# Row-normalising kernel, one core: in the first tile VectorE scales 7 of 12 rows and ScalarE 5, in place of 8 and 4

## The chip, the cores and the metric

The kernel runs on one core of a Trainium2 chip. The metric is the device time of one execution in microseconds (us). Before the change the median was 317.5 us (three runs, 316.85 to 318.54).

## The reference

```python
x = np.random.randn(32, 512, 1024).astype(np.float32)   # seeded

def reference(x):
    sums = np.sum(np.abs(x), axis=-1, keepdims=True)
    return (x / (sums + 1e-8)).astype(np.float32)
```

There are 16,384 rows of 1024 fp32 numbers, each divided by the sum of its absolute values. 67.11 MB are read and 67.11 MB written; every byte is used once.

## The kernel before

The rows go through 11 tiles: ten of 12 rows per partition (6.29 MB each) and a last one of 8. SyncE issues the loads, ScalarE's queue the stores, and four buffers rotate, so the load of tile i+4 waits until the store of tile i has landed (in the trace the load queue waits 229.0 us for stores, in 7 waits). VectorE sums and inverts; the scaling is split, two thirds of a tile's rows to VectorE, one third to ScalarE.

```python
    R = 12
    BUFS = 4
    HEAD = 32
    ...                     # rows = [12] * 10 + [8]; piece(flat, i) is tile i in HBM; tiles 0, 1
                            # and the last share a block that gives each partition 32 adjacent rows
    def normalize(x_tile, r0, k, kv):
        s = stats.tile([P, R], FP32)
        nc.vector.tensor_reduce(out=s[:, :k], in_=x_tile[:, r0 : r0 + k, :],      # L51
            axis=mybir.AxisListType.X, op=mybir.AluOpType.add, apply_absolute_value=True)
        ...                                                   # + EPS (L58), inv = 1/s (L60)
        nc.vector.tensor_mul(                                                     # L61
            out=x_tile[:, r0 : r0 + kv, :], in0=x_tile[:, r0 : r0 + kv, :],
            in1=inv[:, :kv].unsqueeze(2).to_broadcast([P, kv, d]))
        for r in range(kv, k):
            row = x_tile[:, r0 + r, :]
            nc.scalar.activation(out=row, in_=row,                                # L68
                func=mybir.ActivationFunctionType.Copy, scale=inv[:, r : r + 1])

    with tc.manual_schedule():
        for i, k in enumerate(rows):
            x_tile = sbuf.tile([P, R, d], FP32)
            nc.sync.dma_start(out=x_tile[:, :k, :], in_=piece(x_flat, i))         # L78
            normalize(x_tile, 0, k, k - k // 3)
            nc.scalar.dma_start(out=piece(out_flat, i), in_=x_tile[:, :k, :])     # L80
```

Of the kernel before, what the change touches and what calls it, by code (L numbers as in the profile page):

```python
# [1 line left out]

# [4 lines left out]

FP32 = mybir.dt.float32
EPS = 1e-8


@with_exitstack
def kernel(
    ctx: ExitStack,
    tc: tile.TileContext,
    x: bass.AP,
    out: bass.AP,
):
    nc = tc.nc
    P = nc.NUM_PARTITIONS  # L20

    x_flat = x.flatten_outer_dims()
    out_flat = out.flatten_outer_dims()
    n, d = x_flat.shape
# [7 lines that stand above are left out]
    per_partition = n // P  # L32
    assert n % P == 0 and (per_partition - HEAD) % R == 0
    rows = [R] * ((per_partition - HEAD) // R + 2) + [HEAD - 2 * R]

    def piece(flat, i):
        head = flat[: P * HEAD, :].rearrange("(p r) d -> p r d", p=P)
        if i < 2:
            return head[:, R * i : R * (i + 1), :]
        if i == len(rows) - 1:  # L40
            return head[:, 2 * R :, :]
        a = P * (HEAD + R * (i - 2))
        return flat[a : a + P * R, :].rearrange("(p r) d -> p r d", p=P)

    sbuf = ctx.enter_context(tc.tile_pool(name="sbuf", bufs=BUFS))
    stats = ctx.enter_context(tc.tile_pool(name="stats", bufs=4))

    def normalize(x_tile, r0, k, kv):

        s = stats.tile([P, R], FP32)  # L50
        nc.vector.tensor_reduce(  # L51
            out=s[:, :k],
            in_=x_tile[:, r0 : r0 + k, :],
            axis=mybir.AxisListType.X,
            op=mybir.AluOpType.add,
            apply_absolute_value=True,
        )
        nc.vector.tensor_scalar_add(out=s[:, :k], in0=s[:, :k], scalar1=EPS)  # L58
        inv = stats.tile([P, R], FP32)
        nc.vector.reciprocal(out=inv[:, :k], in_=s[:, :k])  # L60
        nc.vector.tensor_mul(  # L61
            out=x_tile[:, r0 : r0 + kv, :],
            in0=x_tile[:, r0 : r0 + kv, :],
            in1=inv[:, :kv].unsqueeze(2).to_broadcast([P, kv, d]),
        )
        for r in range(kv, k):
            row = x_tile[:, r0 + r, :]
            nc.scalar.activation(  # L68
                out=row,
                in_=row,  # L70
                func=mybir.ActivationFunctionType.Copy,
                scale=inv[:, r : r + 1],
            )

    with tc.manual_schedule():
        for i, k in enumerate(rows):
            x_tile = sbuf.tile([P, R, d], FP32)
            nc.sync.dma_start(out=x_tile[:, :k, :], in_=piece(x_flat, i))  # L78
            normalize(x_tile, 0, k, k - k // 3)
            nc.scalar.dma_start(out=piece(out_flat, i), in_=x_tile[:, :k, :])  # L80


# [1 line left out]
_INS = ['x']  # L84
_OUTS = [((32, 512, 1024), 'float32')]


# [23 lines left out]
```

## Time and profile before

| What | Value |
|---|---|
| Median time | 317.5 us |
| Span of the profiled run | 315.6 us |
| VectorE (DVE) busy | 235.8 us, 75% |
| ScalarE (ACT) busy | 46.1 us, 15% |
| Moved by DMA | 134.2 MB, mean 425 GB/s |
| First store issued | 39.96 us |
| First VectorE wait for a load after the start | 3.52 us, before tile 4 |

Read it by asking which resource is never idle. VectorE is the busiest compute engine but idles a quarter of the time; the 16 DMA engines are full from the first load to the last store (a busy share of 0.96 to 1.03 in each stretch of the windows view from 5 to 313 us). The lines are in the prediction below.

### The profile page before, as it was taken

The numbers are of one execution on the slowest core, as the hardware profiler recorded it, in microseconds if no ns is written. First come the engines' busy times: TensorE is split into PE (matmuls) and PEld (weight loads), VectorE is DVE, ScalarE is ACT, GpSimd is POOL, SyncE is SP. The second block draws the span as 40 slices with busy tenths as digits, with TensorE's granted clock in tenths as the row PEclk, the third lists the DMA queues.
The fourth block names the chain that finished last, engine by engine and source line by source line (L and its number), as shares of the span: only waits on it lengthen the run. The fifth ranks groups of instructions, "written<-read, shape, count | busy, mean of one in ns | idle before, by whom it ended". The sixth has DMA issues, their size and how long they took to land.

```text
span 315.6 us, 205 instructions
## 1 busy us (share of the span) xinstructions
DVE 235.8 (75%) x44; ACT 46.1 (15%) x43; POOL 0.2 (0%) x4
## 2 busy tenths in 40 slices
DVE  0079999999999599749937991997499479979300
ACT  0010402204005003100500040031005000502000
POOL 0000000000000000000000000000000000000000
DMA  8999999999999999999999999999999999999996
GB/s 311 486 399 436 461 361 436 399 461 436 399 467 430 411 461 424 430 449 417 461 424 411 461 436 399 461 436 399 467 431 405 467 432 424 436 436 424 455 392 282
DMA packets 3169, 134.23 MB, mean 425 GB/s; under 512 B 352, under 2 KB 352, under 8 KB 352
## 3 DMA queue, kind: packets, MB, share of 16 engines
q1 hardware_dynamic: 1584, 67.11, 49.8%
q10 hardware_dynamic: 1584, 67.11, 49.1%
q14 instruction: 1, 0.01, 0.0%
HBM read 67.11 MB, written 67.11 MB: 425 GB/s over the span
## 4 chain that ended last, share of the span: by engine, by line
another core or an unknown queue 36%; DMA 30%; DVE 26%; SPq 0%; issue 0%; DVEq 0%; ACTq 0%
DMA out_dram<-x_tile 16%; DVE s L51 15%; DMA x_tile<-in_x_dram 15%; DVE x_tile L61 10%; SPq L78 0%; DVE inv L60 0%; DVE s L58 0%; DVEq L60 0%; ACTq L80 0%
## 5 line engine op out<-in xcount | busy, mean ns | idle before, releaser
L51 DVE TENSOR_REDUCE s<-x_tile 128x12 f32<-128x12288 f32 (+1 forms) x11 | 138.2, 12563 | 57.1 <-DMA x_tile<-in_x_dram 57.1
L61 DVE TENSOR_TENSOR x_tile<-x_tile,inv 128x8192 f32<-128x8192 f32 (+1 forms) x11 | 93.5, 8498 | 0.4
L68 ACT ACTIVATE x_tile<-x_tile,inv 128x1024 f32<-128x1024 f32 x42 | 44.9, 1137 | 226.3 <-DVE inv L60 226.3
L68 ACT ACT_TABLE_LOAD x1 | 1.3, 1283 | 17.8 <-DMA x_tile<-in_x_dram 17.8
L60 DVE RECIPROCAL inv<-s 128x12 f32<-128x12 f32 (+1 forms) x11 | 2.5, 226 | 0.9
L58 DVE TENSOR_SCALAR s<-s 128x12 f32<-128x12 f32 (+1 forms) x11 | 1.9, 173 | 0.4
L95 POOL MEMSET const-bfloat16-1.0<- 128x1 bf16 x1 | 0.1, 101 | 0.0
L95 POOL MEMSET const-uint8-127<- 128x1 uint8 x1 | 0.1, 101 | 0.0
L95 POOL MEMSET const-float32-0.0<- 128x1 f32 x1 | 0.1, 98 | 0.2 <-issue 0.2
L95 POOL MEMSET const-float32-1.0<- 128x1 f32 x1 | 0.1, 98 | 0.0
## 6 DMA issues: line engine op xcount, KB each, us to landing
x_tile<-in_x_dram SPq DMA_DIRECT2D x10, 6144.0 KB, 34.0
out_dram<-x_tile ACTq DMA_DIRECT2D x10, 6144.0 KB, 52.4
x_tile<-in_x_dram SPq DMA_DIRECT2D x1, 4096.0 KB, 29.1
out_dram<-x_tile ACTq DMA_DIRECT2D x1, 4096.0 KB, 19.9
```

The source lines that it names most:

```text
L51: nc.vector.tensor_reduce(out=s[:, :k], in_=x_tile[:, r0 : r0 + k, :], axis=mybir.AxisListType.X, op=mybir.AluOpType.add, apply_absolute_v ...
L58: nc.vector.tensor_scalar_add(out=s[:, :k], in0=s[:, :k], scalar1=EPS)
L60: nc.vector.reciprocal(out=inv[:, :k], in_=s[:, :k])
L61: nc.vector.tensor_mul(out=x_tile[:, r0 : r0 + kv, :], in0=x_tile[:, r0 : r0 + kv, :], in1=inv[:, :kv].unsqueeze(2).to_broadcast([P, kv, d]),)
L68: nc.scalar.activation(out=row, in_=row, func=mybir.ActivationFunctionType.Copy, scale=inv[:, r : r + 1],)
L95: nc = _bacc.Bacc("TRN2", target_bir_lowering=False, num_devices=1)
```

## The change

The first store can go only when tile 0 is scaled, and there VectorE needs 8.69 us for 8 rows while ScalarE is done with its four after 4.26. The change gives ScalarE one row more, in tile 0 alone, so that the first store and VectorE's further work start earlier.

```diff
             nc.sync.dma_start(out=x_tile[:, :k, :], in_=piece(x_flat, i))
-            normalize(x_tile, 0, k, k - k // 3)
+
+            normalize(x_tile, 0, k, k - k // 3 - (i == 0))
             nc.scalar.dma_start(out=piece(out_flat, i), in_=x_tile[:, :k, :])
```

## The prediction

> **What bounds the kernel now.** I read the page first, then the trace in windows, then the waits, the chain that ended last, and the timeline around the first and the last tile. The page:
>
> ```profile
> span 315.6 us, 205 instructions
> DVE 235.8 (75%) x44; ACT 46.1 (15%) x43; POOL 0.2 (0%) x4
> DMA  8999999999999999999999999999999999999996
> HBM read 67.11 MB, written 67.11 MB: 425 GB/s over the span
> ```
>
> VectorE is busy for three quarters of the span, but the DMA row shows 9 in all slices except the first and the last. Nothing on a compute engine is that full. The windows view, cut where transfers start or end, says whether those 9s hide gaps (columns: stretch and length, busy time of VectorE, ScalarE and GpSimd, clock, DMA share, GB/s):
>
> ```profile
> 5.00:39.96 34.96, 22.13 (x5) 5.55 (x5) 0.00 (x0) 1.00 0.99 427
> 39.96:50.00 10.04, 10.04 (x1) 0.00 (x0) 0.00 (x0) 1.00 1.03 392
> 50.00:75.00 25.00, 24.86 (x6) 4.26 (x4) 0.00 (x0) 1.00 1.01 436
> 75.00:133.40 58.40, 52.92 (x11) 12.80 (x12) 0.00 (x0) 1.00 1.00 433
> 133.40:191.43 58.03, 44.09 (x8) 8.53 (x8) 0.00 (x0) 1.00 1.00 434
> 191.43:249.51 58.08, 44.09 (x8) 8.54 (x8) 0.00 (x0) 1.00 1.00 433
> 249.51:278.77 29.26, 22.05 (x4) 4.27 (x4) 0.00 (x0) 1.00 1.01 434
> 278.77:294.65 15.88, 15.62 (x4) 2.19 (x2) 0.00 (x0) 1.00 1.02 440
> ```
>
> The DMA engines run at 433 to 434 GB/s whether loads run alone, loads and stores run together, or stores run alone (a short stretch is a few GB/s off because a packet counts whole). The only dip is the 10 us after the first store is issued: (434 - 392) x 10.04 us = 0.42 MB, or 1.0 us of lost transfer time.
>
> The span then adds up. 134.22 MB at 434 GB/s is 309.3 us. The first load lands at 17.70 and its 6.29 MB need 14.5 us, so 3.2 us go at the start. The dip takes 1.0 us. The last landing is at 314.55, so 1.05 us follow it. That makes 314.55; the missing 1.0 us I put, as an estimate, on the delay between the last bytes and their landing. **The bound is bytes through the DMA engines**, and no term of this sum contains VectorE.
>
> The waits, VectorE's and then the load queue's own (total, times, longest):
>
> ```profile
> DVE s L51 <- DMA x_tile<-in_x_dram: 57.1, 8, 17.7
> SPq L78 <- DMA out_dram<-x_tile: 229.0, 7, 57.7
> ```
>
> VectorE idles 57.1 us for loads; the loads idle for stores that must free one of the four buffers. The chain gives the order:
>
> ```profile
> 75.30 8.70 DVE x_tile L61
> ...
> 84.08 49.32 DMA out_dram<-x_tile
> ...
> 249.63 29.12 DMA x_tile<-in_x_dram
> ```
>
> Up to 84.08 this chain runs through VectorE without a gap, tile 0's scaling included. It invites the reading that every microsecond saved there is a microsecond of the span. I don't accept it: the third tile's store, issued at 84.08, takes 49.32 us for bytes that alone need 14.5, because it queues behind the second store and shares the engines with loads.
>
> The timeline of the first tile, the first VectorE wait in mid-kernel, and the end:
>
> ```profile
> 31.18 8.69 DVE L61 TENSOR_TENSOR x_tile<-x_tile,inv 128x8192 f32<-128x8192 f32 x1
> 31.18 4.26 ACT L68 ACTIVATE x_tile<-x_tile,inv 128x1024 f32<-128x1024 f32 x4 [12.12 <-DVE inv L60]
> 39.79 12.94 DVE L51 TENSOR_REDUCE s<-x_tile 128x12 f32<-128x12288 f32 x1
> 39.96 0.37 ACTq L80 DMA_DIRECT2D out_dram<-x_tile  x1
> ...
> 109.57 12.95 DVE L51 TENSOR_REDUCE s<-x_tile 128x12 f32<-128x12288 f32 x1 [3.52 <-DMA x_tile<-in_x_dram]
> ...
> 294.65 0.34 ACTq L80 DMA_DIRECT2D out_dram<-x_tile  x1
> ```
>
> [...] in the middle a load and a store of 6.29 MB each complete every 29.0 us (chain: 28.5 to 28.6 us of transfer plus about 0.5 of issuing), twice 14.5. [...]
>
> **The change part by part.** Only tile 0's split differs.
>
> - VectorE loses one row. The trace has 8692 ns for 8 rows and 6558 for 6, so 1067 ns a row and 7625 for 7. Its scaling ends at 38.80 instead of 39.87.
> - ScalarE gains one ACTIVATE. Four span 4.26 us, so they follow each other every (4.26 - 1.13)/3 = 1.04 us; five span 5.30 and end at 36.48, 2.3 us before VectorE. VectorE still decides when the store may go.
> - Store 0 is issued at about 38.89 instead of 39.96, and the reduce of tile 1 and all VectorE work up to the first load wait (109.57) moves 1.07 us earlier.
>
> What this buys: until 39.96 the loads have the engines alone at full rate (loads 0 to 3 are 25.2 MB, which at 434 GB/s take 58 us). Starting a store 1.07 us earlier moves no byte sooner overall; it gives half of the rate to the store 1.07 us sooner. Loads fall behind by 1.07 x 217 GB/s = 0.23 MB, which at their half rate is 1.07 us. So:
>
> - Store 0 lands 1.07 us earlier (75.4 to 74.3, the trace's semaphore events), and load 4 is issued that much earlier. The load queue gains nothing: by those events load 3 lands only at 80.5, so the queue had 5.1 us of work left anyway.
> - Load 3, then each later load, lands 1.07 us *later*. VectorE reaches tile 4 1.07 us earlier and its data come 1.07 us later: its wait of 3.52 grows to about 5.7.
> - The last load lands at about 279.8 instead of 278.75, and the last store is issued at 295.7. Store 9 lands at 304.8 before (events), so the store queue has some 10 us of backlog when the last store joins it. That covers 1.07 us.
>
> Sum: first-tile chain -1.07, given back as waiting for loads, last-store issue +1.07 inside a 10 us slack; bytes, rate, start, dip and end unchanged: **0.0 us**. The trace's saving is real and lies wholly beside the DMA work.
>
> **The rivals.**
>
> 1. *The chain is right and the saving reaches the end.* For it: no gap on VectorE from 17.72 to 106. Against: the rate of 434 GB/s beside it. It would give 317.5 - 1.1 = 316.4, still within 2%.
> 2. *The later loads reach the end.* If the last store started when issued, the end would move by +1.07, to 318.6. Against: its 19.9 us to landing for 4.19 MB that need 9.7 alone show that it waits in the queue.
> 3. *The dip changes.* The 1.0 us lost when the first store starts is a one-off whose cause I can't see. If the shift doubled or removed it: 316.5 or 318.5.
> 4. *ScalarE becomes the bound of tile 0.* Five ACTIVATEs would have to take over 7.6 us; at 5.30 they do not.
>
> **Range and chances.** The three runs before lie between 316.85 and 318.54, a spread of 1.7 us, more than any rival moves. I predict 317.4: the median, with a tenth for a small chance of rival 1. The range 316.5 to 318.4 is this run-to-run scatter with the rivals inside it. A change of 2% is 6.35 us, six times what the edit touches. Chances: faster 0.01, within 2% 0.98, slower 0.01.
>
> **What would show it right or wrong.** Right: in the changed profile tile 0's scaling is near 7.63 us with five ACTIVATEs in 5.3; the first store is issued near 38.9; VectorE's wait before tile 4 is near 5.7 us and its total wait for loads rises from 57.1 to about 59; the reduce of the last tile starts about 1 us *later*; the GB/s stay at 433 to 434 and the span within half a microsecond. Wrong: loads landing earlier from tile 4 on (then the load queue had a gap that I missed), a span shorter by a whole 1.07 us in every run, or a dip of another size.

The durations are the trace's: one ACTIVATE of 1024 elements takes 1132 to 1149 ns (median 1133, the 1.13 of the second part), VectorE's scaling of 8 rows 8692. With packets that cross a border shared out, the packet records give 433.9 GB/s for loads alone (5 to 39.96), 433.9 for loads and stores together (50 to 75) and 433.8 for stores alone (278.77 to 294.65). The third store, issued at 84.08, does queue behind the second: that one lands at 104.4, and 29.0 us later the third, at 133.4.

## The result, and the profile after

After: 317.06 us median (six runs, 316.74 to 317.46); before, six runs in all: 317.48 (316.85 to 318.54). The ratio is **0.9986, with a 95% interval from 0.9968 to 1.0004**: the same. (A ratio is the mean time of one kernel's fast runs over that of the other's in the same rounds, so not quite the ratio of the medians quoted.) All these runs count as fast: each is within 1.5% of the fastest of its kernel.

The page of the kernel after, VectorE's and the DMA engines' rows:

```profile
DVE 234.7 (74%) x44; ACT 47.2 (15%) x44; POOL 0.2 (0%) x4
DMA  8999999999999999999999999999999999999996
```

VectorE is 1.1 us less busy, ScalarE 1.1 us more, and the DMA row is as it was. The rate in mid-kernel is that of before, too:

```profile
133.40:191.43 58.03, 44.10 (x8) 8.53 (x8) 0.00 (x0) 1.00 1.00 434
```

The timeline of the kernel after, at the places shown before:

```profile
31.12 5.30 ACT L68 ACTIVATE x_tile<-x_tile,inv 128x1024 f32<-128x1024 f32 x5 [12.13 <-DVE inv L60]
31.12 7.62 DVE L61 TENSOR_TENSOR x_tile<-x_tile,inv 128x7168 f32<-128x7168 f32 x1
...
38.83 0.37 ACTq L81 DMA_DIRECT2D out_dram<-x_tile  x1
...
111.17 12.95 DVE L51 TENSOR_REDUCE s<-x_tile 128x12 f32<-128x12288 f32 x1 [6.26 <-DMA x_tile<-in_x_dram]
...
296.24 0.34 ACTq L81 DMA_DIRECT2D out_dram<-x_tile  x1
```

The first store goes 1.13 us earlier (0.06 of that is an earlier first load). VectorE comes to tile 4 earlier, but tile 4's data come 1.60 us *later* than the 109.57 of before, and the last store is issued 1.59 us later than the 294.65 of before. The saving has turned into waiting, as the waits of the kernel after show (total, times, longest):

```profile
DVE s L51 <- DMA x_tile<-in_x_dram: 59.8, 8, 17.7
SPq L78 <- DMA out_dram<-x_tile: 227.6, 7, 55.8
```

VectorE waits 2.7 us more for loads than before (57.1), more than the 1.07 us it saved; the load queue waits less for the first store to land (55.8 against 57.7). By the trace's semaphore events (each transfer has 16 of them at its end, those of store 0 from 72.6 to 75.4 before; it counts as landed with the last) store 0 lands at 73.4 instead of 75.4, load 3 at 82.2 instead of 80.5, the store before the last at 304.8 in both, and the last store at 314.4 instead of 314.5.

### The profile page after: what moved, and what is told of

It is laid out like the page before. It is cut to its first block, busy times and chain, and to the rows that moved or that the text cites. A ratio compares the mean times of both kernels' runs of the same rounds, so it can differ in the third digit from the quotient of the medians.

```text
span 315.5 us, 206 instructions
## 1 busy us (share of the span) xinstructions
DVE 234.7 (74%) x44; ACT 47.2 (15%) x44; POOL 0.2 (0%) x4
## 4 chain that ended last, share of the span: by engine, by line
another core or an unknown queue 36%; DMA 31%; DVE 26%; SPq 0%; issue 0%; DVEq 0%; ACTq 0%
DMA x_tile<-in_x_dram 16%; DMA out_dram<-x_tile 15%; DVE s L51 15%; DVE x_tile L61 10%; SPq L78 0%; DVE inv L60 0%; DVE s L58 0%; DVEq L60 0%; ACTq L81 0%
## 5 line engine op out<-in xcount | busy, mean ns | idle before, releaser
L61 DVE TENSOR_TENSOR x_tile<-x_tile,inv 128x8192 f32<-128x8192 f32 (+2 forms) x11 | 92.4, 8401 | 0.4
L68 ACT ACTIVATE x_tile<-x_tile,inv 128x1024 f32<-128x1024 f32 x43 | 45.9, 1136 | 226.9 <-DVE inv L60 226.9
```

The source lines that it names most:

```text
L61: nc.vector.tensor_mul(out=x_tile[:, r0 : r0 + kv, :], in0=x_tile[:, r0 : r0 + kv, :], in1=inv[:, :kv].unsqueeze(2).to_broadcast([P, kv, d]),)
L68: nc.scalar.activation(out=row, in_=row, func=mybir.ActivationFunctionType.Copy, scale=inv[:, r : r + 1],)
```

## The experiments

Two questions: does the first store's time matter at all, and what would have to be different for it to matter? "Split a/b" is VectorE's and ScalarE's rows of tile 0; the expectations call a run by VectorE's share ("kv12" is e2, "kv1" e3). This table gathers what the runs with four buffers, the kernel's own layout and one first store showed, e4 without computing left out. Store 0 and load 3 are the first store and the fourth load, which share the engines in the stretch from 50 to 80; their landings are from the semaphore events. "Slow" counts, in the trace's records of DMA packets, those of 49,152 bytes that took over 2.0 us, of 2560 (the normal one takes 1.81).

| Kernel | first store issued | store 0 lands | load 3 lands | slow | median us | ratio to before (95%) |
|---|---|---|---|---|---|---|
| before, 8/4 | 39.96 | 75.4 | 80.5 | 36 | 317.5 | 1 |
| after, 7/5 | 38.83 | 73.4 | 82.2 | 42 | 317.06 | 0.9986 (0.9968 to 1.0004) |
| e1, 6/6 | 37.87 | 71.4 | 82.3 | 36 | 317.05 | 1.0001 (0.9983 to 1.002) |
| e5, 9/3 | 41.03 | 75.0 | 81.0 | 40 | 321.15 | 1.0081 (1.0037 to 1.0125) |
| e6, 10/2 | 42.00 | 75.1 | 78.9 | 35 | 317.05 | 0.9987 (0.9975 to 0.9998) |
| e3, 1/11 | 42.79 | 82.6 | 82.4 | 144 | 324.25 | 1.0211 (1.0185 to 1.0237) |
| e2, 12/0 | 44.18 | 81.0 | 80.8 | 120 | 322.1 | 1.0167 (1.0139 to 1.0194) |
| e8, 12/0, no other computing | 44.15 | 81.8 | 81.6 | 155 | 323.46 | 1.0184 (1.0162 to 1.0206) |
| e10, 12/0, load 3 held back | 44.17 | 64.0 | 84.4 | 53 | 319.41 | 1.0052 (1.0016 to 1.0087) |

### e1: twice the change, and e4: no computing at all

```diff
-            normalize(x_tile, 0, k, k - k // 3)
+            normalize(x_tile, 0, k, 6 if i == 0 else k - k // 3)
```

> The first tile split 6 rows to VectorE, 6 to ScalarE: twice the change. From the measured durations VectorE needs 6.56 us and ScalarE 5 x 1.04 + 1.13 = 6.34 us, so the first store goes 2.13 us earlier than before (at 37.8). Theory (bytes through the DMA engines bound the time; an earlier first store only moves rate from loads to stores): ratio to before between 0.997 and 1.001, tile 4's reduce 2 to 3 us later than 109.57 and its wait near 8 us. Rival (the first-tile chain reaches the end; the 0.4 us between the medians of before and after was real and a share of it): 2.13 us off the chain gives 0.993 in full, about 0.9975 if only the seen 40% of it counts.

Measured: 1.0001. Twice the advance gives nothing, so the 0.4 us between the medians of before and after is not the start of a trend. The reduce of tile 4 in e1's timeline:

```profile
111.47 12.95 DVE L51 TENSOR_REDUCE s<-x_tile 128x12 f32<-128x12288 f32 x1 [6.97 <-DMA x_tile<-in_x_dram]
```

It starts 1.90 us later than before, and its wait is 7.0 us, not the 8 expected: store 0 gained 4.0 us, but the loads lost only 1.9.

```diff
-            normalize(x_tile, 0, k, k - k // 3)
```

> All computing taken out; each tile is loaded and stored as it came (the result is wrong on purpose). Measures the time of the bytes alone. Theory (bytes): 315 to 317.5 us, ratio 0.992 to 1.000, although the last 16 us of VectorE work and all of the first chain are gone; the dip at the first store moves to about 18 to 25 us in the span and keeps its 1 us. Rival (the chain through VectorE, 26% of the span, is on the path): clearly below, 0.95 or less.

Measured (result wrong): 316.64 us, ratio 0.9985 (0.9966 to 1.0005). With no VectorE and no ScalarE work the kernel takes the same time to within the noise, at the same rate (here without VectorE's and ScalarE's columns):

```profile
50.00:78.00 28.00, 0.00 (x0) 1.00 1.00 434
```

This is the direct measurement of the bound: the 26% of the chain that lay on VectorE could be taken out whole. By the packet records, the dip came with the first store here too, between 18 and 36 us, and cost 1.1 us; so it belongs to the transfers.

### e2 and e3: the first store later

```diff
-            normalize(x_tile, 0, k, k - k // 3)
+            normalize(x_tile, 0, k, 12 if i == 0 else k - k // 3)     # e2; in e3: 1 in place of 12
```

> The first tile scaled by VectorE alone (12 rows, 12.96 us): the first store and all VectorE work behind it come 4.27 us later than before. Theory (bytes): loads come 4 to 6 us earlier from tile 2 on, VectorE has no wait before tile 4 (it gets there at 110.3), the load queue runs dry for some us before load 4 but the store queue has work then, so the engines stay full and the ratio is 0.998 to 1.003. Rival (chain): 317.5 + 4.3, ratio 1.0134. Rival (the dry load queue costs its gap): 1.005 to 1.02.

> The first tile split 1 row to VectorE, 11 to ScalarE. This parts the two things that the change moves together: VectorE is free 7.5 us earlier (about 32.4), while ScalarE (11 x 1.04 + 0.09 = 11.5 us) lets the first store go only at about 42.8, 2.8 us later than before. Theory (bytes): ratio 0.998 to 1.003. Rival (VectorE chain): minus 7.5 us, ratio 0.976. Rival (the first store's time decides): plus 2.8 us, ratio 1.009.

Measured: 1.0167 and 1.0211. My theory, in the form "only bytes count, so a shift either way is free", fell. Neither rival of e3 fits: VectorE 7.5 us ahead did not save 7.5 us, and the first store 2.8 us late cost 6.9. In e2 the chain rival's 4.3 us looks right by size (4.7 measured), but the windows view says otherwise. Before, then e2:

```profile
50.00:78.00 28.00, 27.79 (x8) 6.96 (x7) 0.00 (x0) 1.00 1.01 435
78.00:95.00 17.00, 17.00 (x2) 1.56 (x2) 0.00 (x0) 1.00 1.00 434
```

```profile
50.00:78.00 28.00, 27.90 (x5) 4.27 (x4) 0.00 (x0) 1.00 1.00 400
78.00:95.00 17.00, 16.90 (x5) 4.26 (x4) 0.00 (x0) 1.00 0.98 402
```

The share of busy DMA engines (the column before the last) is 1.00 and 0.98: the engines did not idle. They moved 400 instead of 434 GB/s, which over these 45 us is 28 x 35/435 + 17 x 32/434 = 3.5 us of the 4.7. By the packet records 120 packets took over 2 us instead of 36, which is 3.2 us more for each engine on average, and the engines then end less evenly. In e3 the same stretches show 390 and 399 GB/s. What e2 was expected to show between also failed: load 2 came earlier (46.8 instead of 51.5), but the load queue as a whole was dry for only 0.2 us (load 3 landed at 80.8, though on seven engines by 76.0, and load 4 was issued at 81.05), and VectorE did wait before tile 4, for 5.94 us. The lost time comes from slower packets, not from a gap or from VectorE.

### e5 and e6: where does it begin?

The edit is that of e2 with 9 and with 10.

> First tile 9 rows to VectorE, 3 to ScalarE: the change with its sign turned; the first store comes 1.07 us later than before, at about 41.0. After kv12 and kv1 the plain theory of bytes alone has fallen for a later store: there the engines stay busy but move 390 to 400 GB/s instead of 434 between 50 and 95. Theory A (a cliff: packets are slow only when the first store begins after the second-last of the first four loads, load 2, has landed at 46.8, so that load 3 and store 0 begin together; in before its first packets run beside load 2's last): 0.999 to 1.003 here. Theory B (slope: each us of delay of the first store costs about 1.1 us, from 4.7 for 4.27): 1.0037.

> First tile 10 rows to VectorE, 2 to ScalarE: first store 2.13 us later, at about 42.1. Theory A (cliff): load 2 all but over when the first store's packets start, so either still 1.00 or already most of the 4.7 to 6.9 us of kv12 and kv1 (1.010 to 1.02), with the rate of 50 to 95 down to 400; not between. Theory B (slope): 1.0075.

Measured: e6 0.9987, e5 1.0081. Both theories missed. There is no slope (2.0 us later costs nothing), and no clean edge in the store's time either, since 1.07 us later cost more than 2.0 us later. e5 is uneven: its runs took 320.32, 321.96, 321.37, 320.93, 323.42 and 316.73 us; two of these were set aside as slow only for being over 1.5% above the fastest, with all of them at the full clock. Its profiled run (320.32) kept full rate in the stretch from 50 to 95. The time is lost at the end; the last two stretches of e5 in the windows view:

```profile
314.00:316.00 2.00, 0.00 (x0) 0.00 (x0) 0.00 (x0) 1.00 0.04 16
316.00:318.60 2.60, 0.00 (x0) 0.00 (x0) 0.00 (x0) 1.00 0.03 13
```

A share of 0.03 to 0.04 is less than one of 16 engines. Following packets from end to start, one engine had eight slow packets where others had two or three (5.6 us of excess against 1.5 to 2.1), and the tail goes with one engine: most engines end their last packet by 313.5, as before, while one engine's worth of packets ends at 314.9, 316.1 and 317.3. In the kernel before no packet starts after 314 but one stray record (the last packets end at 314.2). So the same kind of slowing hit one engine alone. (Which packets belong to one engine is a reconstruction from their times; it gives each engine about 176 packets, in e5 the lagging one too, so there the others did not relieve it.)

### e7, e8, e9: what are the slow packets?

```diff
-        head = flat[: P * HEAD, :].rearrange("(p r) d -> p r d", p=P)     # e7, besides the edit of e2:
-        if i < 2:                                                          # every tile contiguous
-            return head[:, R * i : R * (i + 1), :]
+        a = P * R * i
         if i == len(rows) - 1:
-            return head[:, 2 * R :, :]
-        a = P * (HEAD + R * (i - 2))
+            return flat[a:, :].rearrange("(p r) d -> p r d", p=P)
```

> kv12 with all tiles laid out alike: tile i is a contiguous piece of the tensor (rows of a partition 48 KB apart) instead of the first two and the last tile interleaved at 128 KB from partition to partition. Theory A1 (the slow packets come from where store 0 and load 3 lie in HBM): 1.000 to 1.004, rate of 50 to 95 back near 434. Theory A2 (they come from the order of the queues alone, whatever the addresses): 1.012 to 1.018 as for kv12.

Measured: 325.95 us, ratio 1.0273 (1.0232 to 1.0314). The result fits neither theory. The rate is near what A1 expected: 439 GB/s from 50 to 78 and 411 from 78 to 95 (425 and 428 when packets that cross a border are shared out), with 71 slow packets in place of 120. The time is longer than that of e2, so most of its loss lies elsewhere: the second store lands on 13 engines by 98.1 us, but on the other three at 102.7, 103.0 and 108.7. So e7 doesn't exclude the addresses as a cause of the slow packets. The contiguous layout with the split 8/4 was not run, so how much of the 2.7% is the layout's own stays open.

```diff
-            normalize(x_tile, 0, k, k - k // 3)
+            if i == 0:                                 # e8
+                normalize(x_tile, 0, k, k)
```

> No computing but in tile 0, which VectorE alone scales: the first store goes at about 44.2 as in kv12, the others follow at once, and no engine works beside the DMA from 44.2 on (wrong result on purpose). Theory (slow packets are a matter of transfers alone): rate from 50 to 95 clearly below 434 and 1.007 to 1.02. Rival (they need VectorE or ScalarE traffic in SBUF beside them): rate near 434 and ratio 0.997 to 1.003.

Measured (wrong): 1.0184. The windows of e8:

```profile
50.00:78.00 28.00, 0.00 (x0) 0.00 (x0) 1.00 1.01 395
78.00:95.00 17.00, 0.00 (x0) 0.00 (x0) 1.00 0.99 399
```

No engine computes here and the DMA engines are full, yet they move 395 to 399 GB/s. The slow packets are a matter of the transfers alone.

```diff
-            nc.scalar.dma_start(out=piece(out_flat, i), in_=x_tile[:, :k, :])
+            if i == 0:                                 # e9, besides the edit of e2
+                o = piece(out_flat, i)
+                nc.scalar.dma_start(out=o[64:], in_=x_tile[64:, :k, :])
+                nc.scalar.dma_start(out=o[:64], in_=x_tile[:64, :k, :])
+            else:
+                nc.scalar.dma_start(out=piece(out_flat, i), in_=x_tile[:, :k, :])
```

> kv12 with the first tile's store issued as two stores of 64 partitions, the upper half first, so that the packets of store 0 no longer meet the packets of load 3 for the same partitions in the same order. In the records of kv12 load 3 is 0 to 1 packets ahead of store 0 on most DMA engines and store packets take 2.4 to 2.5 us instead of 1.8; in the kernel before the store is 2 packets ahead of the load and every packet takes 1.8. Theory P (like-numbered packets of load and store meet): rate of 50 to 78 back to about 434, ratio 1.000 to 1.006. Rival Q (the order does not matter, a load and a store that begin together are enough): rate near 400, ratio 1.012 to 1.02.

Measured: 325.6 us, ratio 1.0258 (1.0242 to 1.0274), 377 GB/s from 50 to 78 and 344 from 78 to 95. Theory P fell: by the edit, the packets of the two queues no longer met for the same partitions, and the loss grew; there were 153 slow packets. Rival Q is not refuted, though the loss is larger than it expected.

### e10: the order turned round

```diff
+        if after_sum is not None:                      # in normalize, after the reduce; besides the edit of e2
+            nc.vector.memset(after_sum[:, 0, 0:1], 0.0)
 ...
-            normalize(x_tile, 0, k, 12 if i == 0 else k - k // 3)
+            normalize(x_tile, 0, k, 12 if i == 0 else k - k // 3, first[3] if i == 1 else None)
```

(The first four tiles are allocated ahead, as `first`; load 3 must wait for the memset into its buffer.)

> kv12 with load 3 held back (its buffer is touched by VectorE after tile 1's sums, at about 57) so that store 0 has begun 4 packets or more ahead of it. Theory (the load-before-store order at the start makes the slow packets): no slow stretch after 57, rate of 57 to 95 near 434; the price is up to 2 us of idle engines between the end of load 2 (46.8) and the first store packets, so 1.002 to 1.008. Rival (a later first store is dear in itself): 1.012 to 1.018 or more.

Measured: 1.0052, inside the theory's range and below the rival's. The windows of e10:

```profile
50.00:78.00 28.00, 27.90 (x6) 4.26 (x4) 0.00 (x0) 1.00 1.00 430
78.00:95.00 17.00, 16.90 (x5) 4.27 (x4) 0.00 (x0) 1.00 1.03 445
```

The first store is issued as late as in e2 and VectorE's work is as late; only load 3 now begins well behind store 0. The rate is back and with it most of the loss. So a late first store is not dear in itself. But load 3 was held back further than planned: its first packets start at 61.2, when store 0's are all but done (its last full ones end between 61.2 and 61.7). So e10 changed the order and also took the two transfers apart, and doesn't show that the order is what counts. The expected 2 us of idle engines did not come about (the first store packets started at 45.9, before load 2 landed at 46.7); what remained of the loss was again one engine ending late (its last store landed at 317.4).

### e11 and e12: where the engines do idle

```diff
-    BUFS = 4
+    BUFS = 2          # e11; e12 has the edit of e2 as well
```

> Two buffers instead of four, split 8 and 4 everywhere. Control: load i+2 must wait for store i, so the DMA engines run dry while VectorE works. All theories: slower, 1.05 to 1.25, DMA share of the span below 0.95. Needed as the base of the next run.

> Two buffers and the first tile scaled by VectorE alone: first store 4.27 us later than in the run with two buffers and 8 and 4. Theory (a shift of the first store reaches the end where the engines have idle time and the waits are closed into a loop): 2 to 5 us longer than that run, that is 0.006 to 0.015 of the before's time more in its ratio. Rival (later stages absorb it): less than 1 us longer.

Measured: 367.52 us (ratio 1.1582) and 370.6 us (1.1674). The windows from 40 to 50, e11 and then e12:

```profile
40.00:50.00 10.00, 10.00 (x2) 0.00 (x0) 0.00 (x0) 1.00 0.91 393
```

```profile
40.00:50.00 10.00, 10.00 (x2) 1.28 (x1) 0.00 (x0) 1.00 0.55 236
```

Here the DMA engines wait for the first store: the delay of 4.05 us (issued at 44.16 instead of 40.11) shows as idle engines (a share of 0.55 against 0.91), and 370.6 - 367.5 = 3.1 us of it reach the end. In this case the first store's time counts, as far as a later one shows it; an earlier one was not run with two buffers. With four buffers the kernel is not in it. (e11 and e12 show 248 and 253 slow packets, with store 0 landing long before load 3: the count alone is no sign of the state of e2.)

## Why the prediction was right

That the time lies in the range says little, since the range held the rivals too. The evidence is in the trace and in e1 and e4.

- **The bound.** The prediction said bytes through the DMA engines, with no term for VectorE. Right for this change: e4 without computing is at 0.9985. Its accounting at a constant 434 GB/s (the trace's rate from 50 to 278) was too simple for other shifts, as e2, e3 and e8 showed. The 1.0 us that its sum lays on the landing is not there: the last packet ends at 314.2, 0.3 us before it. By the packet records the dip is 0.2 us larger than it took, and the engines end unevenly, between 312.9 and 314.2.
- **The cost of the two edits.** Right: VectorE 7.62 us (predicted 7625 ns), five ACTIVATEs in 5.30 us, first store at 38.83 (predicted 38.89). Rival 4 is out: ScalarE ended 2.3 us before VectorE.
- **The saving turns into waiting.** Right in kind: loads later, VectorE's wait before tile 4 longer, last reduce and last store later, end unchanged. The size was off: loads moved by 1.60 us, not 1.07, store 0 landed 1.95 us earlier, not 1.07, and the wait is 6.26, not about 5.7. My term let the store take its share from its issue on, and as a smooth half. In the records its earliest packet starts 5.2 us after the issue before and 4.4 after, at 45.13 and 43.27, 1.86 us apart. Later the two queues take turns by packets of 49,152 bytes and 1.81 us (in chains of packets, reconstructed as for e5, each of the 86 packets that start between 60 and 72 before and have a successor there is followed by one of the other queue), and these shifts are near one packet; that the step is one packet is my reading of the records, not tested by itself.
- **The slack at the end.** Right: the last store joined the queue at 296.24, with the store before it landing at 304.8; nothing reached the end.
- **Rival 1** (the chain reaches the end) is refuted by e1 and e4. **Rival 2** (later loads reach the end) did not happen. **Rival 3** (the dip): from 40 to 50 the rate was 393 GB/s before and after (and in e1, e2 and e3), and by the packet records the dip cost 1.2 us before and 1.3 after.
- **What the prediction did not see.** It took a shift of the first store as harmless in either direction as long as the engines stay full. e2, e3 and e8 lost 1.7 to 2.1% with full engines. In the table, every kernel in which store 0 landed before load 3 shows 35 to 53 slow packets, and every one in which load 3 landed first (by 0.2 us) shows 120 or more. e10 held load 3 back, and the slow stretch went away. That the way in which these two transfers meet decides is thus shown; that it is their order is not, since e10 took them apart as well. The change itself moves away from this region: its store 0 lands further ahead of load 3 (8.7 us against 5.1).
- **What speaks against the order alone.** In e2, load 3 begins first on all 16 engines, but only nine of them have the slow stretch. In the chains of packets (reconstructed as for e5) it begins on these nine one packet ahead of store 0, and four to six packets from there to 80 us are slow. On the other seven it is two or more packets ahead, and one or two are slow. The landings show the same two groups without a reconstruction: load 3 lands on seven engines at 75.5 to 76.0, on nine at 79.3 to 80.8. The number of packets is no rule either: load 3 was two ahead on 15 engines in e7 and in e9, and 13 of these had no slow packet up to 80 us in e7, while all 15 had three to six in e9. In e4, store 0 begins beside load 1, and load 1 (44.3) lands before store 0 (51.5) without slow packets.
- **What stays open.** Why packets slow down is not known: the compute engines (e8) and the meeting of like partitions (e9) are excluded, addresses (e7) are not. Also open is why a single engine lags in e5 and e10.

No version tried beats both kernels: e1 is within noise of them, e6 is at most 0.25% below the kernel before (interval 0.9975 to 0.9998), and even e4, without computing, saves less than 1 us.

## What to carry to other kernels

Before shortening work ahead of a transfer, look whether the DMA engines are already full beside it. Here they were (before, shares of 1.00 to 1.03 from 39.96 to 133.40): with the first store issued 1.13 us earlier the data of tile 4 came 1.60 us later, and the 1.07 us that VectorE saved came back as 2.7 us more of waiting. A chain view that runs through a compute engine doesn't prove that the engine is the bound: 26% of the chain lay on VectorE, and taking the computing out (e4, ratio 0.9985) was a cheap test that showed it was not. And a full DMA share was not yet full rate: e2 had a share of 1.00 at 400 GB/s, the kernel before 1.01 at 435, so read the GB/s beside it.
